# A two-layer decoder trunk on one core: some feed forward input products issued 128 tokens wide instead of 256

## The chip, the cores and the metric

The kernel runs on one core of one Trainium2 chip. The metric is the device time of one execution in microseconds (us). Before the change two executions took 2003.5 and 1999.16 us, with a median of 2001.33 us.

## What is computed

The input is a residual stream of 256 tokens with 2048 features in float32. Layer 0 adds a gated linear recurrence block (RG-LRU) and then a SwiGLU feed forward block. One key and value projection is then taken from the stream, and layer 1 adds a sliding window attention block that uses it, and another SwiGLU block. This case is about the SwiGLU blocks, of which there are two:

```python
D_MODEL = 2048
D_FF = ((8 * D_MODEL // 3 + 255) // 256) * 256      # 5632

def swiglu_ffn(x, g, w_in, w_out):
    h = rms_norm(x, g)
    gate, up = jnp.split(h @ w_in, 2, axis=-1)
    return x + (jax.nn.silu(gate) * up) @ w_out
```

Everything is float32, and every large product is weights (features by features) times the 256 tokens.

## The kernel before

**Layout.** The stream is kept transposed: features on the 128 partitions, the 256 tokens along the free axis. A product therefore holds a 128 by 128 block of weights in TensorE (VectorE, ScalarE and TensorE are named DVE, ACT and PE in the profile) and streams the tokens past it, and the result, 128 features by 256 tokens, accumulates in one PSUM bank of 512 columns.

**Three products instead of one.** A float32 operand is split in two numbers of the type float32r: `hi`, a rounded copy, and `lo`, what the rounding left. A product is then the sum of three: weights `hi` times tokens `hi`, weights `hi` times tokens `lo`, and weights `lo` times tokens `hi`. An activation slot is a tile of 512 columns, with the `hi` half of the 256 tokens in columns 0 to 255 and the `lo` half in columns 256 to 511. The letters of the table `PARTS` (line 259) name such a product: each gives whether the weights are `hi` (1) or `lo` (0), and which columns of the slot are streamed. `a` is `hi` weights with `hi` tokens, `b` is `hi` weights with `lo` tokens, `l` is `lo` weights with `hi` tokens, each 256 columns wide. `h` is `a` and `b` in one instruction of 512 columns; its two halves land in the two halves of the bank and are added when the bank is emptied.

**Jobs and chunks.** All weights come from HBM in one list of jobs, in the order of use. A job is a chunk of 128 by 1024 numbers (512 KB): two blocks of input features (`k`) by four blocks of output features (`f`), so eight blocks of weights. `stream` (line 244) runs over the jobs. For job `i` it issues the DMA of the chunk four jobs ahead (`load`, from the SP queue), splits the chunk three jobs ahead into `hi` (ACT, line 241) and `lo` (DVE, line 242), and then issues the products of job `i`. Four buffers each for the raw chunk, `hi` and `lo` take turns.

**Groups.** `group` (line 273) makes the jobs of four banks that accumulate together. For the feed forward input there are 22 groups in each of the two layers, and each group has eight chunks, `c` from 0 to 7, because its contraction runs over 2048 features. For each chunk, `group` writes the list `todo` of products as triples of `k`, `f` and the letter. In chunks 0, 2 and 5 (`SYNC`) some `a` and `b` pairs are an `h`. In chunk 7 the products are sorted by bank, so that the first bank is done early. In chunks 1, 3, 4 and 6 the list has `a` and `b` for each of the eight blocks, and then `l` for each of the eight: 24 products of 256 columns.

**Issue.** `products` (line 261) turns the list into instructions. Each entry is one matmul call, and the build makes of each call a weight load (LDWEIGHTS, the profile's engine row PEld) and a MATMUL (row PE). Halfway through the list it calls `half_tick` once.

**The rest of the work.** Normalization, SiLU, splitting of activations, attention and the like run as generators in the background. `run_bg` issues their steps at the ticks, so many per tick as budgets of estimated DVE and ACT time allow; these budgets and the ticks do not depend on how many products a chunk has. `done` empties a group's banks with `pull` after chunk 7. The output projection of the feed forward (`project`) uses `group` as well.

The lines that matter here:

```python
                if not self.started:
                    self.started = True
                    todo = [(k, f, p) for k in range(2) for q in ("ab", "l") for f in range(4) for p in q]
                elif c == nk // 2 - 1:
                    todo = [(k, f, p) for f in range(4) for k in range(2) for p in "abl"]
                else:
                    run = [(0, 0), (1, 0), (0, 1)] if c in sync else []
                    todo = [(k, f, p) for k, f in both if (k, f) not in run for p in "ab"]
                    ...
                    todo += [(k, f, "l") for k, f in both]
```

Of the kernel before, what the change touches and what calls it, by code (L numbers as in the profile page):

```python
# [17 lines left out]
P = 128  # L18
D = 2048
T = 256  # L20
DFF = 5632
ND = D // P
NH = DFF // P
# [25 lines left out]
class Trunk:  # L49
# [206 lines left out]
            self.run_bg()  # L256
        self.drain()

    PARTS = {"h": (1, 0, 2 * T), "a": (1, 0, T), "b": (1, T, 2 * T), "l": (0, 0, T)}

    def products(self, todo, ps, hi, lo, x2, begun, last):


        for n, (k, f, p) in enumerate(todo):
            if 2 * n in (len(todo), len(todo) + 1):
                self.half_tick()
            high, c0, c1 = self.PARTS[p]
            w = (hi if high else lo)[:, k * 512 + f * P:k * 512 + f * P + P]
            self.nc.tensor.matmul(ps[f][:, 0:c1 - c0], w, x2[k][:, c0:c1], start=f not in begun,  # L269
                                  stop=last and all(q[1] != f for q in todo[n + 1:]))  # L270
            begun.add(f)

    def group(self, src, nk, xs, done, last=False, sync=()):


        st = {}
        both = [(k, f) for k in range(2) for f in range(4)]
        for c in range(nk // 2):
            def mm(hi, lo, c=c):
                if c == 0:  # L280
                    st["ps"] = [self.bank() for _ in range(4)]
                    st["begun"] = set()
                x2 = [self.need(xs[2 * c + kt]) for kt in range(2)]
# [3 lines that stand above are left out]
                elif c == nk // 2 - 1:  # L287

                    todo = [(k, f, p) for f in range(4) for k in range(2) for p in "abl"]
                else:  # L290
                    run = [(0, 0), (1, 0), (0, 1)] if c in sync else []
                    todo = [(k, f, p) for k, f in both if (k, f) not in run for p in "ab"]
                    at = sync.index(c) if run else 0
                    todo[at:at] = [(k, f, "h") for k, f in run]
                    todo += [(k, f, "l") for k, f in both]
                self.products(todo, st["ps"], hi, lo, x2, st["begun"], c == nk // 2 - 1)
                if last:
                    for q in x2:
                        self.free(q)
                if c == nk // 2 - 1:  # L300
                    done([(p, bool(sync) and f < 2) for f, p in enumerate(st["ps"])])
            self.jobs.append((src(c), mm))
# [111 lines left out]
    def ffn(self, l, xs, r, gains, rn, out=None):  # L414
        hid = [Val() for _ in range(NH)]
        w = self.d[f"ffn_in{l}"]
        for g in range(NH // 2):
            def done(ps, g=g):
                rs = self.rstd[r][:, 0:T]
                early = not self.rv[r].ready  # L420
                v = [self.pull(p, r=None if early else rs) for p in ps]

                def task():
                    while not self.rv[r].ready:
                        yield 1
                    for h in range(2):
                        ga, up = v[2 * h], v[2 * h + 1]
                        if early:
                            self.tt(ga, ga, rs, ALU.mult)
                            self.tt(up, up, rs, ALU.mult)  # L430
                        self.a(ga, ga, AF.Silu)
                        yield
                        self.tt(ga, ga, up, ALU.mult)
                        while not self.slots:
                            yield 1
                        s = self.slot()
                        self.split_act(s, ga)
                        self.free_half(ga)
                        self.free_half(up)
                        hid[2 * g + h].ap = s  # L440
                        hid[2 * g + h].ready = True
                        yield
                self.spawn(task())
            self.group(lambda c, g=g: w[g, c], ND, xs, done, g == NH // 2 - 1, self.SYNC)
        self.project(self.d[f"ffn_out{l}"], NH, hid, gains, rn, out)


# [562 lines left out]
```

## Time and profile before

| what | value |
|---|---|
| median of two runs | 2001.33 us (1999.16 to 2003.5) |
| the profiled execution, its own time | 1999.26 us |
| its span, first to last instruction | 1997.5 us |
| PE busy | 1987.8 us, 16795 matmuls |
| PEld busy | 1955.1 us, 16795 weight loads |
| DVE busy | 1282.1 us (64%) |
| ACT busy | 1077.6 us (54%) |
| granted TensorE clock | 1.000 |
| line 269 (`products`) | 15927 of the matmuls: 10423 with `hi` weights, 5504 with `lo` weights |

The profile is of one execution on the chip. A matmul record of PE begins when the instruction starts to stream, and its end is modelled, so that records of neighbours overlap: a matmul of 256 columns is shown with 276 ns, though the next one starts after less than half of that. The number to read is therefore the distance from one start to the next. A row of the timeline merges neighbours of the same kind: it gives the start, the time from the first start to the last end, and how many there are; the distance is that time less one record, divided by the count less one. A window row gives for each engine the busy time and the number of instructions in a stretch of the span.

### The profile page before, as it was taken

The numbers are of one execution on the slowest core, as the hardware profiler recorded it, in microseconds if no ns is written. First come the engines' busy times: TensorE is split into PE (matmuls) and PEld (weight loads), VectorE is DVE, ScalarE is ACT, GpSimd is POOL, SyncE is SP. The second block draws the span as 40 slices with busy tenths as digits, with TensorE's granted clock in tenths as the row PEclk, the third lists the DMA queues.
The fourth block names the chain that finished last, engine by engine and source line by source line (L and its number), as shares of the span: only waits on it lengthen the run. The fifth ranks groups of instructions, "written<-read, shape, count | busy, mean of one in ns | idle before, by whom it ended". The sixth has DMA issues, their size and how long they took to land.

```text
span 1997.5 us, 40277 instructions
## 1 busy us (share of the span) xinstructions
PE 1987.8 (100%) x16795; PEld 1955.1 (98%) x16795; DVE 1282.1 (64%) x2062; ACT 1077.6 (54%) x1624; POOL 0.2 (0%) x4
## 2 busy tenths in 40 slices
PE   8999999999999999999999999999999999999999
PEld 8999999999999999999999999999999999999999
DVE  8989867556556656545768786765565566554543
ACT  7798655445444444434556775554454454444342
POOL 0000000000000000000000000000000000000000
PEclk9999999999999999999999999999999999999999
DMA  7655655655656566566564335655655665666663
GB/s 268 199 183 177 202 195 188 196 191 190 200 191 197 193 192 198 191 193 197 192 189 141 122 116 169 191 194 191 195 191 195 195 195 191 195 195 202 206 204 128
DMA packets 105015, 376.58 MB, mean 189 GB/s; under 512 B 11648, under 2 KB 13824, under 8 KB 104832
## 3 DMA queue, kind: packets, MB, share of 16 engines
q1 hardware_dynamic: 104832, 374.01, 58.1%
q8 instruction: 131, 2.15, 0.4%
q14 instruction: 52, 0.43, 0.1%
HBM read 371.86 MB, written 2.10 MB: 187 GB/s over the span
## 4 chain that ended last, share of the span: by engine, by line
PE 99%; ACT 0%; DMA 0%; DVE 0%; issue 0%
PE b L269 94%; PE b L545 1%; PE b L832 1%; PE b L740 1%; PE b L895 0%; PE b L851 0%; PE b L784 0%; PE b L786 0%; PE b L785 0%; PE b L853 0%; PE b L852 0%; PE b L749 0%; PE b L750 0%; PE b L751 0%; DMA x<-in_x 0%; ACT hi L241 0%
## 5 line engine op out<-in xcount | busy, mean ns | idle before, releaser
L269 PE MATMUL b<-s,hi 128*128 128x256 f32 (+1 forms) x10423 | 1430.2, 284 | 6.6 <-ACT hi L241 5.7
L269 PEld LDWEIGHTS b<-s,hi 128*128 128x128 f32 x10423 | 1322.5, 188 | 33.9 <-ACT hi L241 6.0
L242 DVE TENSOR_TENSOR lo<-raw,hi 128x1024 fp32r<-128x1024 f32 (+1 forms) x705 | 861.0, 1222 | 661.6 <-ACT hi L241 658.1
L241 ACT ACTIVATE hi<-raw 128x1024 fp32r<-128x1024 f32 (+1 forms) x705 | 746.1, 1059 | 774.7 <-PE b L269 744.3
L269 PE MATMUL b<-s,lo 128*128 128x256 f32 x5504 | 824.4, 277 | 0.0
L269 PEld LDWEIGHTS b<-s,lo 128*128 128x128 f32 x5504 | 716.4, 188 | 0.0
L105 ACT ACTIVATE t<-b 128x256 f32<-128x256 f32 x130 | 48.8, 384 | 62.2 <-PE b L269 37.9
L105 ACT ACTIVATE h<-h 128x256 f32<-128x256 f32 (+1 forms) x104 | 38.9, 375 | 21.1 <-DVE h L114 21.1
L105 ACT ACTIVATE s<-h 128x256 fp32r<-128x256 f32 (+1 forms) x106 | 42.7, 413 | 13.4 <-DVE h L114 10.9
L105 ACT ACTIVATE s<-s 128x256 f32<-128x256 f32 (+1 forms) x112 | 41.2, 415 | 4.0 <-DVE s L118 3.3
L114 DVE TENSOR_TENSOR h<-b,rstd 128x256 f32<-128x256 f32 x102 | 41.6, 415 | 0.0
L105 ACT ACT_TABLE_LOAD x31 | 39.8, 1283 | 1.3 <-PEq L1000 0.7
L114 DVE TENSOR_TENSOR h<-h,rstd 128x256 f32<-128x256 f32 x92 | 38.3, 420 | 1.5
L118 DVE SCALAR_TENSOR_TENSOR s<-x,par,s 128x256 fp32r<-128x256 f32 x80 | 36.7, 479 | 3.9 <-ACT s L105 3.9
L105 ACT ACTIVATE s<-x,par 128x256 fp32r<-128x256 f32 x80 | 37.9, 497 | 2.3 <-DVE x L114 1.8
L114 DVE TENSOR_TENSOR h<-b,t 128x256 f32<-128x256 f32 x90 | 37.5, 417 | 0.0
L114 DVE TENSOR_TENSOR s<-s,s 128x256 fp32r<-128x256 f32 (+1 forms) x80 | 31.0, 419 | 8.8 <-ACT s L105 8.6
L114 DVE TENSOR_TENSOR s<-h,s 128x256 fp32r<-128x256 f32 x88 | 36.6, 417 | 0.0
L114 DVE TENSOR_TENSOR h<-h,h 128x256 f32<-128x256 f32 x88 | 36.4, 415 | 0.1
L105 ACT ACTIVATE s<-b 128x384 f32<-128x384 f32 (+3 forms) x70 | 28.4, 428 | 10.3 <-PE b L853 5.6
L105 ACT ACTIVATE s<-s,h 128x128 f32<-128x128 f32 x64 | 28.3, 444 | 6.2 <-DVE h L123 6.2
L114 DVE TENSOR_TENSOR x<-x,b 128x256 f32<-128x256 f32 x64 | 25.2, 415 | 8.9 <-PE b L269 8.9
(99 smaller groups left out, 610.4 us busy)
## 6 DMA issues: line engine op xcount, KB each, us to landing
raw<-in_ffn_in SPq DMA_DIRECT2D x352, 512.0 KB, 3.5
raw<-in_ffn_out SPq DMA_DIRECT2D x176, 512.0 KB, 4.2
raw<-in_lru_in SPq DMA_DIRECT2D x63, 512.0 KB, 3.8
raw<-in_lru_out SPq DMA_DIRECT2D x32, 512.0 KB, 3.4
raw<-in_w_q SPq DMA_DIRECT2D x32, 512.0 KB, 3.3
raw<-in_w_o SPq DMA_DIRECT2D x32, 512.0 KB, 3.5
raw<-in_gate SPq DMA_DIRECT2D x8, 512.0 KB, 4.0
raw<-in_kv SPq DMA_DIRECT2D x8, 512.0 KB, 4.3
```

Source lines behind the costliest of these rows:

```text
L105: self.nc.scalar.activation(out, in_, func, **kw)
L114: self.nc.vector.tensor_tensor(out, a, b, op)
L118: self.nc.vector.scalar_tensor_tensor(out, a, s, b, op0, op1)
L241: self.nc.scalar.activation(hi[:, q], raw[:, q], AF.Copy)
L242: self.nc.vector.tensor_tensor(lo[:, q], raw[:, q], hi[:, q].bitcast(F32), ALU.subtract)
L269: self.nc.tensor.matmul(ps[f][:, 0:c1 - c0], w, x2[k][:, c0:c1], start=f not in begun, stop=last and all(q[1] != f for q in todo[n + 1:]))
L545: nc.tensor.matmul(ps[j][:, 0:T], (hi if high else lo)[:, c:c + P], x2[kt][:, q:q + T], start=kt == 0 and high > q, stop=kt == 1 and not high)
L740: nc.tensor.matmul(ps[f][:, 0:T], w0, x2[kt][:, q:q + T], start=k0 + kt == 0 and high > q, stop=k0 + kt == ND - 1 and not high)
L832: nc.tensor.transpose(p[:, j * P:(j + 1) * P], sc[hh][:, j * P:(j + 1) * P], one)
```

## The change

Ten letters stand in `PARTS` for products now. `p`, `q`, `r` and `s` are `hi` weights with the first and second 128 tokens of the `hi` half (`p`, `q`) and of the `lo` half (`r`, `s`). `m` and `n` are `lo` weights with the first and second 128 tokens of the `hi` half. `products` writes a narrow product to the half of the bank's columns that its tokens belong to (`o0`).

`FORMS` holds six orders. A form is a tuple of strings; for each string the eight blocks are gone through, and for each block the letters of the string. In chunks 1, 3 and 6 of each feed forward input group the list `todo` is made from a form; which one is `(g + l) % 6`, with the group `g` and the layer `l`. Chunks 0, 2, 4, 5 and 7, and all other stages, keep their lists. The same sums are computed.

```diff
-    PARTS = {"h": (1, 0, 2 * T), "a": (1, 0, T), "b": (1, T, 2 * T), "l": (0, 0, T)}
+    PARTS = {"h": (1, 0, 2 * T), "a": (1, 0, T), "b": (1, T, 2 * T), "l": (0, 0, T),
+             "p": (1, 0, P), "q": (1, P, T), "r": (1, T, T + P), "s": (1, T + P, 2 * T), "m": (0, 0, P), "n": (0, P, T)}
+
+    FORMS = (("pqrsmn",), ("ambn",), ("ab", "mn"), ("a", "m", "b", "n"), ("armns",), ("ab", "m", "n"))
 
     def products(self, todo, ps, hi, lo, x2, begun, last):
...
             high, c0, c1 = self.PARTS[p]
             w = (hi if high else lo)[:, k * 512 + f * P:k * 512 + f * P + P]
-            self.nc.tensor.matmul(ps[f][:, 0:c1 - c0], w, x2[k][:, c0:c1], start=f not in begun,
+            o0 = c0 % T
+            self.nc.tensor.matmul(ps[f][:, o0:o0 + c1 - c0], w, x2[k][:, c0:c1], start=f not in begun,
                                   stop=last and all(q[1] != f for q in todo[n + 1:]))
...
-    def group(self, src, nk, xs, done, last=False, sync=()):
+    def group(self, src, nk, xs, done, last=False, sync=(), form=None):
...
                     todo = [(k, f, p) for f in range(4) for k in range(2) for p in "abl"]
+                elif form is not None and c in (1, 3, 6):
+                    todo = [(k, f, p) for q in self.FORMS[form] for k, f in both for p in q]
                 else:
...
-            self.group(lambda c, g=g: w[g, c], ND, xs, done, g == NH // 2 - 1, self.SYNC)
+            self.group(lambda c, g=g: w[g, c], ND, xs, done, g == NH // 2 - 1, self.SYNC, (g + l) % 6)
```

## The prediction

> **What bounds the kernel now.** I read the page's shares and chain first, then who PE waited for, then windows over the two stages that the diff touches, and last the timeline inside one chunk.
>
> ```profile
> span 1997.5 us, 40277 instructions
> PE 1987.8 (100%) x16795; PEld 1955.1 (98%) x16795; DVE 1282.1 (64%) x2062; ACT 1077.6 (54%) x1624; POOL 0.2 (0%) x4
> PEclk9999999999999999999999999999999999999999
> PE 99%; ACT 0%; DMA 0%; DVE 0%; issue 0%
> PE b L269 94%; PE b L545 1%; PE b L832 1%; PE b L740 1%; PE b L895 0%; PE b L851 0%; PE b L784 0%; PE b L786 0%; PE b L785 0%; PE b L853 0%; PE b L852 0%; PE b L749 0%; PE b L750 0%; PE b L751 0%; DMA x<-in_x 0%; ACT hi L241 0%
> ```
>
> The chain that ended last is PE for 99%, and line 269, the products, for 94%. The clock is full throughout.
>
> ```profile
> L269 PE MATMUL b<-s,hi 128*128 128x256 f32 (+1 forms) x10423 | 1430.2, 284 | 6.6 <-ACT hi L241 5.7
> L269 PE MATMUL b<-s,lo 128*128 128x256 f32 x5504 | 824.4, 277 | 0.0
> L241 ACT ACTIVATE hi<-raw 128x1024 fp32r<-128x1024 f32 (+1 forms) x705 | 746.1, 1059 | 774.7 <-PE b L269 744.3
> L242 DVE TENSOR_TENSOR lo<-raw,hi 128x1024 fp32r<-128x1024 f32 (+1 forms) x705 | 861.0, 1222 | 661.6 <-ACT hi L241 658.1
> ```
>
> These groups show the direction of waiting: PE stood idle 6.6 us before the products of `hi` and not at all before those of `lo`, while ACT waited 744.3 us for PE to give back `hi` buffers.
>
> Windows over the two input stages (columns: busy us and count for PE, PEld, DVE, ACT, POOL; then clock, DMA share, GB/s):
>
> ```profile
> 281.50:759.30 477.80, 477.80 (x4013) 469.61 (x4012) 293.02 (x407) 238.20 (x315) 0.00 (x0) 1.00 0.60 194
> 1258.00:1735.40 477.40, 477.40 (x4007) 469.19 (x4006) 292.36 (x405) 237.69 (x314) 0.00 (x0) 1.00 0.60 194
> ```
>
> In these two windows, together 955.2 us, PE has no idle time, DVE is busy 61%, ACT 50%, the DMA engines 60%. Nothing but the pace of PE's own instructions sets the time there. That pace is read from one chunk, PE's timeline (start, us from first start to last end, count):
>
> ```profile
> 802.38 1.07 PE L269 MATMUL b<-s,lo 128*128 128x256 f32 x8
> 803.29 1.98 PE L269 MATMUL b<-s,hi 128*128 128x256 f32 x16
> 805.10 1.07 PE L269 MATMUL b<-s,lo 128*128 128x256 f32 x8
> ```
>
> From the first `lo` product of one chunk to that of the next are 805.10 − 802.38 = 2.72 us, and 24 products: **113.3 ns a step** at 256 columns. As a check, the stage: 44 groups of 8 chunks of 2.72 us are 957 us, the length of the two windows.
>
> **The change part by part.**
>
> *How many products.* A chunk before has 24, all 256 wide. Form 0 (`pqrsmn`) has 48, all 128 wide: 24 more. Form 4 (`armns`) has 8 wide and 32 narrow: 16 more. Forms 1, 2, 3 and 5 have 16 wide and 16 narrow: 8 more. Over the 22 groups of layer 0 and, shifted by one, of layer 1, the forms 0 to 5 come 7, 8, 8, 8, 7 and 6 times, in three chunks each. Added instructions: 3 × (7×24 + 8×8 + 8×8 + 8×8 + 7×16 + 6×8) = 3 × 520 = **1560**. Each is the second half of a product that was whole, so 1560 steps of 256 columns go and 3120 of 128 columns come; the columns streamed are the same. The change costs 3120 × t − 1560 × 113.3 ns = 3120 × t − 176.8 us, and all hangs on t, the step of a narrow product.
>
> *The step t.* The trace has no float32r product narrower than 256, so t is bounded by rows. If a step took only as long as its columns, it would be half of 113.3: 56.7 ns. But every matmul carries its own weight load: the page counts 16795 of both, although an `a` and the `b` behind it use the same block, so repeated weights are loaded again. What a load costs shows where almost nothing is streamed, at line 895, two columns against 128 columns of weights (timeline of PEld), and, in the groups by shape, in the records of loads:
>
> ```profile
> 1106.00 1.87 PEld L895 LDWEIGHTS b<-con,s 128*128 128x128 f32 x16
> ...
> L269 PEld LDWEIGHTS b<-s,lo 128*128 128x128 f32 x5504 | 716.4, 188 | 0.0
> L832 PEld LDWEIGHTS b<-con,s 128*128 128x128 f32 x96 | 11.3, 140 | 0.9 <-issue 0.5 <-DVE s L114 0.2
> L853 PEld LDWEIGHTS b<-s,s 128*64 128x64 f32 x64 | 7.9, 137 | 0.0
> L895 PEld LDWEIGHTS b<-con,s 128*128 128x128 f32 x64 | 7.5, 191 | 0.0
> ```
>
> Sixteen loads in 1.87 us with a record of 0.19 us: (1.87 − 0.19) / 15 = **112 ns from load to load**, for products of two columns. So the load alone holds PE to one matmul in 112 ns. Its record, 191 ns, is that of the products' loads, 188 ns; a load of 64 columns at line 853 has 137 ns, which gives (188 − 137) × 2 = 102 ns for the part that grows with 128 columns. At 256 columns the stream (113.3) just hides the load (112); at 128 columns the stream (57) hides half of it, and the load sets the step. Line 895 works on plain float32 and the products on float32r, which is why this remains an estimate; the equal records are my reason to carry it over. I take **t = 112 ns**. The low end of this reading is 102 ns. The high end is 117 ns, the pace of wide products while attention runs beside them (six distances in 0.98 − 0.28 us):
>
> ```profile
> 1105.30 0.98 PE L269 MATMUL b<-s,hi 128*128 128x256 f32 x7
> ```
>
> The sum: 3120 × 112 ns = 349.4 us, less 176.8, **+172.6 us**. The ends: +141 at 102 ns, +188 at 117 ns.
>
> The Trainium skill, "TensorE: Matmul & The Clock Gate", section "LDWEIGHTS (loading the stationary operand)", puts a load at its column count over 1.2 GHz whatever the contraction, so 107 ns for 128 columns; the trace's 112 is a little longer. By the Trainium skill's figure the sum would be +157 us and the time 2156, as an estimate.
>
> *Does anything hide it?* PE has no idle time in these windows for the extra steps to fall into, so all of it lies on the path.
>
> *Order of `hi` and `lo`.* Forms 0, 1, 3 and 4 mix `lo` and `hi` weights. A `lo` block is then wanted from the second to the ninth or so product on, instead of the 17th, and the `hi` buffer is read nearly to the end of the chunk. The split three chunks ahead hides both. Within the chunk above:
>
> ```profile
> 802.58 1.06 ACT L241 ACTIVATE hi<-raw 128x1024 fp32r<-128x1024 f32 x1 [1.66 <-PE b L269]
> ...
> 803.67 1.23 DVE L242 TENSOR_TENSOR lo<-raw,hi 128x1024 fp32r<-128x1024 f32 x1 [1.50 <-ACT hi L241]
> ```
>
> ACT refills a `hi` buffer just after its last product and DVE is done with `lo` at 804.90; three whole chunks (8.2 us) lie between the chunk that gave the buffer back, which ended at 803.29, and the one that needs it, at about 811.4. Release up to 0.9 us later, at the end of the chunk, leaves some 5 us. I cost it at nothing. Behind ACT's waiting split stand the background's activations and the bank evictions, and DVE's subtraction; if the cover were gone, each us late would be one us on PE in each of up to 132 chunks. A longer chunk widens the cover.
>
> *The rest.* `half_tick` still runs once in mid list, so ACT, DVE and SP get the same instructions in the same order, with no DMA added or moved; no new kind of wait arises. Transfers are needed less often, and the 60% DMA share falls. 3120 more PE instructions must be fetched; the fetch queues now move 2.6 MB for 40277 instructions, 64 bytes each, so 0.2 MB more, which I cost at nothing:
>
> ```profile
> q8 instruction: 131, 2.15, 0.4%
> q14 instruction: 52, 0.43, 0.1%
> ```
>
> **The forecast**: the profiled execution took 1999.26 us (1.8 around the span), 2 us under the median of the two runs and inside their spread. 1999.3 + 172.6 = **2172 us**.
>
> **The rivals.**
>
> 1. *The load is hidden even behind 128 columns* (not slower). A float32r load may take half of a float32 one: the only loads of 128 columns with a shorter record, 140 ns, are line 832's transposes. If a load takes 57 ns or less, t is 56.7 and the time 1999. It decides from t = (176.8 + 40) / 3120 = 69.5 ns: below it, the change is within 2% (40 us), which is about what a measurement of this kernel can tell from no change. Against it speaks the 188 ns record of the products' own loads. Chance 0.09. The Trainium skill, "TensorE: Matmul & The Clock Gate", section "Back-to-back issue gap", gives a width formula that puts 55.8 ns at 128 columns; by it the time would be 1997.
>
> 2. *The load is hidden in part*, t midway between 57 and 112, so 84.5 ns: 263.6 − 176.8 = +87, 2086 us. For it: no row shows float32r below 256. Against: line 895 would have to be slow for its type. Chance 0.03. The Trainium skill, in the section just named, has sustained pairs of load and matmul at about 81 ns for 128 columns, without saying the type; by that figure it would be +76, 2075.
>
> 3. *A load of weights already in the array costs nothing*, only a change of block does. A step is 112 where the next product takes another block and 57 or 113 else. Per block before 340 ns; form 0 adds 4×57 + 2×112 − 340 = 112 ns, forms 1, 3 and 5 add 110, form 2 55, form 4 166. Times 168 blocks for form 0, 528 for forms 1, 3 and 5, 192 for form 2 and 168 for form 4: 19 + 58 + 11 + 28 = +116, 2115 us. The wide pairs of today would hide it; that each has its own load record speaks against it. Chance 0.03.
>
> 4. *Load and stream no longer overlap at 128 columns*: t = 112 + 57 = 169, +350, 2350 us. At 256 columns they overlap fully, or the step would be 225. Chance 0.03.
>
> 5. *The change does not reach the chip as written*, the build joining neighbours: 1999 us. The `a` and `b` of today, adjacent and of one block, stay two. Chance 0.01.
>
> **How the numbers follow.** Forecast 0.80, rivals 0.09, 0.03, 0.03, 0.03, 0.01, and 0.01 for a gain, for which I see no row: 40 us would need t below 44 ns, less than the stream alone. The forecast's bounds run from 1999 + 141 = 2140 to 1999 + 188 = 2187; I add the 4 us by which the two runs differ and some margin for steps above 117 where wide and narrow alternate, 2200. The 0.20 outside are the rivals, so the range stays 2140 to 2200. Slower by over 2%: 0.80 + 0.03 + 0.03 + 0.03 = 0.89; within: 0.09 + 0.01 = 0.10; faster 0.01.
>
> **What would show it.** In the changed profile: 18355 matmuls; the two input stages longer by some 86 us each, all other stages as before; PE without idle time there; narrow loads following each other every 112 ns. A changed chunk, 2.72 us now, takes 48 × 112 = 5.38 us in form 0, 8 × 113.3 + 32 × 112 = 4.49 in form 4, 3.61 in the others. Rival 3 shows as form 2 shorter than form 5. I would be wrong if narrow products followed each other at well under 100 ns or over 125, or if idle time before products came up, from the earlier use of `lo`.

## The result, and the profile after

The changed kernel took 2198.34 us (2198.17 and 2198.51 in two runs) against 2001.33: a ratio of **1.0991, 95% interval 1.0973 to 1.1008**, slower by 197 us. The profiled execution took 2198.17 us.

From the page of the changed kernel (line 274 is line 269 of before):

```profile
span 2196.4 us, 43409 instructions
PE 2185.6 (100%) x18355; PEld 2151.6 (98%) x18355; DVE 1282.0 (58%) x2062; ACT 1071.6 (49%) x1624; POOL 0.2 (0%) x4
PEclk9999999999999999999999999999999999999999
PE 99%; ACT 1%; DMA 0%; DVE 0%; issue 0%; SPq 0%; DVEq 0%; ACTq 0%
L241 ACT ACTIVATE hi<-raw 128x1024 fp32r<-128x1024 f32 (+1 forms) x705 | 745.6, 1058 | 994.3 <-PE b L274 937.8
```

PE bounds the kernel as it did, at the full clock. There are 1560 more matmuls and as many more weight loads; DVE and ACT have the same 2062 and 1624 instructions in nearly the same busy time. ACT waits longer for PE (937.8 us, 744.3 before), so the cover of the splits has grown. Groups by shape:

```profile
L274 PE MATMUL b<-s,hi 128*128 128x256 f32 x9334 | 1358.7, 282 | 7.8 <-ACT hi L241 6.9 <-ACT s L105 0.8
L274 PE MATMUL b<-s,lo 128*128 128x256 f32 x4448 | 689.6, 278 | 0.0
L274 PE MATMUL b<-s,lo 128*128 128x128 f32 x2112 | 342.9, 263 | 0.0
L274 PE MATMUL b<-s,hi 128*128 128x128 f32 x1008 | 184.8, 265 | 0.0
```

The narrow products are 2112 + 1008 = 3120, and PE waited for no operand before them. Windows over the two input stages, each from its first product to the first of the next stage (columns as in the prediction):

```profile
299.60:879.90 580.30, 580.30 (x4827) 571.49 (x4826) 294.02 (x408) 236.74 (x317) 0.00 (x0) 1.00 0.54 160
1376.00:1953.60 577.60, 577.60 (x4803) 568.80 (x4802) 293.20 (x406) 236.70 (x315) 0.00 (x0) 1.00 0.54 161
```

PE is still without a gap. The stages are 580.3 and 577.6 us long; between the same two products before they were 480.3 and 480.6. Together that is 960.9 to 1157.9 us, **+197.0: nearly the whole loss is there**. The two profiled executions are 198.9 us apart, and what the stages leave of it, 1.9 us, is less than the 4.3 us between the two executions before. One changed chunk of form 5 and its neighbours, timeline of PE and the loads of the same narrow row:

```profile
516.60 2.04 PE L274 MATMUL b<-s,hi 128*128 128x256 f32 x16
518.49 1.90 PE L274 MATMUL b<-s,lo 128*128 128x128 f32 x16
```

```profile
518.37 1.87 PEld L274 LDWEIGHTS b<-s,lo 128*128 128x128 f32 x16
```

Sixteen narrow loads take 1.87 us, (1.87 − 0.19) / 15 = **112 ns apart**, as line 895's were before. Over all narrow products of the trace that follow a narrow one, the distance is 111.6 ns. This leaves out the first distance of each row: the second record begins only 58 ns after the first. In turn the second wide product behind a row begins about 170 ns after the first one. Together that is what two full steps take, so I read it as records that begin early, before their weights are in; the trace does not show this by itself. But the sixteen wide products take 2.04 us where they took 1.98: (2.04 − 0.28) / 15 = **117 ns instead of 113.3**. That was not foreseen, and it is not confined to the changed chunks. Mean distance from the first product of a chunk to that of the next, in us, worked out from the traces (chunks in which the background adds matmuls left out):

| chunk | 0 | 1 | 2 | 3 | 4 | 5 | 6 | 7 |
|---|---|---|---|---|---|---|---|---|
| before | 2.73 | 2.72 | 2.73 | 2.72 | 2.72 | 2.73 | 2.72 | 2.72 |
| after, form 0 | 2.80 | **5.31** | 2.87 | **5.31** | 2.88 | 2.75 | **5.31** | 2.88 |
| after, form 4 | 2.81 | **4.47** | 2.87 | **4.47** | 2.88 | 2.75 | **4.46** | 2.88 |
| after, form 5 | 2.82 | **3.62** | 2.87 | **3.62** | 2.88 | 2.82 | **3.62** | 2.88 |

The bold chunks are the changed ones. Chunks whose instructions are the same as before grew too. A part of that is bookkeeping: a chunk behind a narrow one begins about 55 ns early, and its time has that more. The rest is wide products at the slower pace. In the input stages 4786 wide steps take 117.8 ns, where before 165 did; that is 4621 × 4.46 ns = 20.6 us, and the 396 products of 512 columns rose from 228.9 to 231.8 ns, 1.1 us.

### The profile page after: what moved, and what is told of

The parts are those of the page before. It is cut to its first block, busy times and chain, and to the rows that moved or that the text cites. A ratio compares the mean times of both kernels' runs of the same rounds, so it can differ in the third digit from the quotient of the medians.

```text
span 2196.4 us, 43409 instructions
## 1 busy us (share of the span) xinstructions
PE 2185.6 (100%) x18355; PEld 2151.6 (98%) x18355; DVE 1282.0 (58%) x2062; ACT 1071.6 (49%) x1624; POOL 0.2 (0%) x4
## 4 chain that ended last, share of the span: by engine, by line
PE 99%; ACT 1%; DMA 0%; DVE 0%; issue 0%; SPq 0%; DVEq 0%; ACTq 0%
PE b L274 94%; PE b L552 1%; PE b L839 1%; PE b L747 1%; PE b L902 0%; PE b L858 0%; PE b L791 0%; DMA raw<-in_lru_in 0%; PE b L793 0%; PE b L792 0%; PE b L860 0%; ACT hi L241 0%; PE b L859 0%; PE b L756 0%; PE b L757 0%; PE b L758 0%
## 5 line engine op out<-in xcount | busy, mean ns | idle before, releaser
L274 PE MATMUL b<-s,hi 128*128 128x256 f32 (+2 forms) x10927 | 1601.8, 287 | 7.8 <-ACT hi L241 6.9
L274 PEld LDWEIGHTS b<-s,hi 128*128 128x128 f32 x10927 | 1442.2, 188 | 36.4 <-ACT hi L241 7.3
L241 ACT ACTIVATE hi<-raw 128x1024 fp32r<-128x1024 f32 (+1 forms) x705 | 745.6, 1058 | 994.3 <-PE b L274 937.8
L274 PE MATMUL b<-s,lo 128*128 128x256 f32 (+1 forms) x6560 | 1031.3, 273 | 0.0
L274 PEld LDWEIGHTS b<-s,lo 128*128 128x128 f32 x6560 | 891.1, 189 | 0.0
```

Source lines behind the costliest of these rows:

```text
L241: self.nc.scalar.activation(hi[:, q], raw[:, q], AF.Copy)
L274: self.nc.tensor.matmul(ps[f][:, o0:o0 + c1 - c0], w, x2[k][:, c0:c1], start=f not in begun, stop=last and all(q[1] != f for q in todo[n + ...
```

## The experiments

Two questions were open: whether the weight load is really what sets the narrow step, and where the slow wide steps come from. All ratios are against the kernel before on the same chip.

**Is it the load? Fewer tokens per product.**

```diff
-            self.nc.tensor.matmul(ps[f][:, o0:o0 + c1 - c0], w, x2[k][:, c0:c1], ...)
+            d = 64 if c1 - c0 == P else c1 - c0
+            for j in range(0, c1 - c0, d):
+                self.nc.tensor.matmul(ps[f][:, o0 + j:o0 + j + d], w, x2[k][:, c0 + j:c0 + j + d], ...)
```

> Every narrow product is cut once more, into two of 64 tokens, each with its own load of 128 weight columns (6240 instead of 3120, the same sums). If the weight load sets the step, 64 tokens cost what 128 cost, about 111 ns: 3120 more steps, +346 us on the changed kernel's 2198, so 2545 us. Rival: a narrow float32r product streams its tokens at half the pace of a wide one, so that its columns set the step: two of 64 tokens together take what one of 128 took, and the time stays at 2198 us.

It took 2816.7 us in its one execution. The chunks of forms 1 and 3 take 5.36 us, which is 16 × 113.3 + 32 × 111 ns, and the loads of a row (timeline of PEld) stand as far apart as for 128 tokens:

```profile
650.92 3.66 PEld L276 LDWEIGHTS b<-s,lo 128*128 128x128 f32 x32
```

(3.66 − 0.19) / 31 = 112 ns, for half the columns. The rival, a slower stream, is out. But the time is 270 us over what the load rule gave, for another reason: the granted clock. Its mean was 0.897. A chunk of form 0, 96 products of 64 tokens, window and timeline:

```profile
796.50:812.50 16.00, 16.00 (x90) 16.00 (x89) 1.42 (x2) 0.22 (x1) 0.00 (x0) 0.59 0.22 66
```

```profile
797.22 1.06 PE L276 MATMUL b<-s,hi 128*128 128x64 f32 x8
798.11 0.61 PE L276 MATMUL b<-s,lo 128*128 128x64 f32 x4
...
800.32 1.89 PE L276 MATMUL b<-s,hi 128*128 128x64 f32 x8
802.03 1.04 PE L276 MATMUL b<-s,lo 128*128 128x64 f32 x4
```

From 797.22 to 798.11 eight products pass, 111 ns each; from 800.32 to 802.03 eight take 214 ns each. In the clock record of this trace 60 stretches, each a whole multiple of 3.41 us and 580 us together, run at half clock. 580 / 2 = 290 us is the excess; without it the time would be about 2527, near the 2545 of the load rule. The step nearly doubled at half the clock (111 to 214 ns), so the load goes with PE's clock. The Trainium skill, "TensorE: Matmul & The Clock Gate", section "Part 1: The HAM clock gate (the "warmup" mystery)", has a gate that halves the clock after an idle window of about 3.4 us; the length and the half agree with this trace. The idleness does not: here PE had no gap in its records, only 64 columns streamed in the time of 256.

**Is it the load? Fewer weight columns per product.**

```diff
-            self.nc.tensor.matmul(ps[f][:, o0:o0 + c1 - c0], w, x2[k][:, c0:c1], ...)
+            d = 64 if c1 - c0 == P else P
+            for j in range(0, P, d):
+                self.nc.tensor.matmul(ps[f][0:d, o0:o0 + c1 - c0], w[:, j:j + d], x2[k][:, c0:c1], ...)
```

> Every narrow product is issued twice, each time with the first 64 of its 128 weight columns (the other 64 output features are left out and the first 64 are added twice, so the output is not the reference's; the instructions are as many as in the run with 64 tokens). If the weight load sets the step, half a load takes 56 ns and the stream 57, so the pair costs what one narrow product cost: 2198 us, up to 2230 if something is added per instruction. Rivals: columns streamed at half pace, or a fixed price per product, give 111 ns for each, 2545 us.

(The text above is not exact: the second call takes the second 64 weight columns, and adds their result to the first 64 rows of the bank. The sizes are as stated.) It took 2247.54 us in its one execution, 17 us above the top of what was expected, with 6240 narrow products, as many as in the run with 64 tokens. Timeline of PEld, a row of 32:

```profile
528.70 2.04 PEld L276 LDWEIGHTS b<-s,lo 128*64 128x64 f32 x32
```

(2.04 − 0.135) / 31 = 61 ns: half the load, nearly half the step. Half a load (56 ns) and the stream of 128 tokens (57) are too close to say which of them now sets it, and the 3 or 4 ns above both are not explained. Most of the 49 us over the changed kernel's 2198 come from forms 1 and 4, in which a narrow product stands before a wide one. There the wide product's full load has only 57 ns to hide behind: in form 1 a block is 113.3 + 60 + 112 + 113.3 + 60 + 112 = 571 ns, times eight 4.57 us, and 4.58 was measured; in form 4 it is 113.3 + 7 × 60 + 112, times eight 5.16, and 5.16 was measured. So a step is the longer of the stream of one product and the load of the **next**. That settles the price of the narrow products.

**Does one narrow product slow the wide ones?**

```diff
-                elif form is not None and c in (1, 3, 6):
-                    todo = [(k, f, p) for q in self.FORMS[form] for k, f in both for p in q]
+                elif form is not None and c == 1:
+                    todo = [(k, f, p) for k, f in both for p in "ab"] + [(0, 0, "m"), (0, 0, "n")]
+                    todo += [(k, f, "l") for k, f in both[1:]]
```

> As before the change, but in chunk 1 of each feed forward input group one product (weights lo, the first block) is cut into two of 128 tokens: 44 cuts, which by themselves cost 44 x 0.111 = +5 us. Theory: a narrow product leaves PE's wide products at 117.7 instead of 113.3 ns until three products of 512 columns in chunk 5 bring the pace back. Then 75 wide steps a group are slow, 0.33 us, and +15 us come on top: 2021 us (2043 if chunk 5 does not bring it back). Rival: the slow wide steps of the changed kernel come from the mass of narrow work or from what runs beside it, not from one narrow product: 2006 us.

2004.6 us, ratio 1.0025 (1.0016 to 1.0035): +5 us. My theory missed and the rival was right. Chunk 1 takes 2.83 us, 0.11 more, and the chunks behind it 2.72 to 2.73, as before the change. A single pair of narrow products leaves the pace alone.

**Does the slow pace end by itself?**

```diff
-            self.group(lambda c, g=g: w[g, c], ND, xs, done, g == NH // 2 - 1, self.SYNC)
+            self.group(lambda c, g=g: w[g, c], ND, xs, done, g == NH // 2 - 1)
```

> As before the change, no narrow product, but without the products of 512 columns in the feed forward input groups (two of 256 in place of each; the banks are then emptied without the second half). Theory: the slow pace lasts until a 512 product ends it. Layer 0 enters its input stage at the fast pace and keeps it; layer 1 enters it at the slow pace, left by the attention, and keeps it for all 22 groups, 192 x 22 x 4.4 ns = +18 us: 2019 us. Rival: the pace comes back by itself, or depends on what runs beside: 2000 us in both layers.

2035.13 us, ratio 1.0175 (1.0158 to 1.0192): +35 us with no narrow product in it. The windows over the middle of both input stages:

```profile
327.00:777.00 450.00, 450.00 (x3823) 450.00 (x3823) 250.68 (x322) 195.72 (x240) 0.00 (x0) 1.00 0.59 187
1320.00:1770.00 450.00, 450.00 (x3823) 450.00 (x3823) 250.59 (x320) 195.25 (x240) 0.00 (x0) 1.00 0.59 187
```

3823 products in 450 us are 117.7 ns each, in both layers. The pace persists, and in the kernel before it is the products of 512 columns that end it; I was wrong to think that layer 0 would be spared. Its timeline shows where the slow pace begins, in the first group, and that it still holds in the last one:

```profile
309.84 1.98 PE L269 MATMUL b<-s,hi 128*128 128x256 f32 x16
...
313.93 0.59 PE L372 MATMUL b<-acc,con 128*128 128x256 f32 x2
314.36 0.50 PE L374 MATMUL b<-con,acc 128*128 128x1 f32 x4
...
792.98 1.10 PE L269 MATMUL b<-s,lo 128*128 128x256 f32 x8
```

Before the norm's six small products the wide ones take (1.98 − 0.28) / 15 = 113 ns; after them, and to the end of the stage, (1.10 − 0.28) / 7 = 117 ns. So the pace is no property of narrow products: a passage of other products can bring it about, and it stays.

**Does the order of the same products matter?** Three runs in which all forms are one: single pairs (two wide, two narrow for each block), fours (four wide, four narrow), and rows of sixteen. Their three edits stand in one block, with comments added:

```diff
-    FORMS = (("pqrsmn",), ("ambn",), ("ab", "mn"), ("a", "m", "b", "n"), ("armns",), ("ab", "m", "n"))
+    FORMS = (("abmn",),) * 6           # single pairs
+    FORMS = (("ab", "mn"),) * 6        # rows of sixteen
...
+                    todo = [(k, f, p) for i in range(0, 8, 2) for q in ("ab", "mn") for k, f in both[i:i + 2] for p in q]   # fours
```

> The changed kernel with one order in place of the six forms: for each block the wide products a and b, then its two narrow products m and n. 16 narrow products a changed chunk, 132 such chunks, 1056 added products. The load rule gives one added step of about 113 ns each, +120 us. Theory of the pace: what the wide products take afterwards depends on the sum of the steps before them; the single pair of the run with one cut took 57 + 114 + 169 = 340 ns up to the next wide start but one, three wide steps exactly, and left the pace at 113.3. So with single pairs the unchanged chunks stay at 2.72 us: 2119 us. Rival: eight narrow pairs in a chunk slow the wide products in any order: 2146 us, like the run that goes with this one.

> The changed kernel with form 2 alone: all wide products of the chunk, then the sixteen narrow ones in a row. The same products as in the run with single pairs, in another order. Theory of the pace: the row of sixteen leaves the wide products at 117.7 ns, so that the unchanged chunks take 2.81, 2.87, 2.88, 2.82 and 2.88 us, 0.63 us a group more than before, 28 us in all: 2146 us. Rival: the order is of no account, and both runs take the same time.

> The changed kernel with one order for all groups, between the run with single pairs and the run with rows of sixteen: two blocks at a time, four wide products and then their four narrow ones. The same products as in both. If what counts is that a narrow passage adds up to whole wide steps: the two steps more, 111 and 113 ns, are 2.7 ns short of two steps of 113.3, and the question is whether the fast pace bears that. If it does, 2118 us as with single pairs; if it does not, the wide products behind run at 117.7 ns in the changed chunks too, 2140 us as with rows, up to 2150.

| order | time, us | ratio (interval) | chunks 0 to 7, medians, us |
|---|---|---|---|
| pairs | 2118.79 | 1.0586 (1.0571 to 1.0600) | 2.73 3.57 2.78 3.57 2.78 2.73 3.57 2.78 |
| fours | 2140.09 | 1.0697 (1.0681 to 1.0713) | 2.81 3.63 2.80 3.61 2.88 2.75 3.61 2.88 |
| rows | 2140.04 | 1.0690 (1.0676 to 1.0705) | 2.81 3.62 2.86 3.62 2.88 2.75 3.55 2.88 |

The same 1056 added products cost 21 us more in rows and fours than in pairs. Chunk 4, which is the same in all, on the timelines of pairs (first) and rows (second):

```profile
532.91 2.03 PE L274 MATMUL b<-s,hi 128*128 128x256 f32 x16
534.78 1.07 PE L274 MATMUL b<-s,lo 128*128 128x256 f32 x8
```

```profile
536.24 2.10 PE L274 MATMUL b<-s,hi 128*128 128x256 f32 x16
538.17 1.10 PE L274 MATMUL b<-s,lo 128*128 128x256 f32 x8
```

Its eight `lo` products take (1.07 − 0.28) / 7 = 113 ns behind pairs and (1.10 − 0.28) / 7 = 117 behind rows. A pair added 113.3 ns (a group 24.50 us, before 21.78, and 2.72 / 24 = 0.1133). The passage of a pair (57 + 114 + 169 ns) is exactly three fast steps; with four, two of 111 to 113 come in between, a little off, and the pace is lost. That the sum of steps is what counts is the reading that led to these runs, and it foretold pairs and rows.

The traces allow a closer look at it: the time from the last wide product before a narrow row to the second one behind it, in fast steps of 113.33 ns. Pairs take 4.00 steps and keep the fast pace; the first fours of a chunk take 5.98, and the pace is slow behind the last. Rows of 8, 16 and 48 that turned the fast pace into the slow one take 9.92, 17.80 and 49.33. In the run with half the weight columns, the first row of sixteen in a chunk of form 3 takes 10.93 and turns the pace slow, and the second takes 11.01 and turns it fast again. One case does not fit: form 4 of that run has rows of 7.32 steps with a single wide product between them, and the chunks behind are at the fast pace. So the reading stays a likely one, and why the wide products have two paces is not shown by it.

**Can the 512 products bring it back?**

```diff
                     run = [(0, 0), (1, 0), (0, 1)] if c in sync else []
+                    if form is not None and c in (0, 2, 4):
+                        run = both
                     todo = [(k, f, p) for k, f in both if (k, f) not in run for p in "ab"]
-                    at = sync.index(c) if run else 0
+                    at = sync.index(c) if c in sync else 0
...
-                    done([(p, bool(sync) and f < 2) for f, p in enumerate(st["ps"])])
+                    done([(p, bool(sync) and f < (2 if form is None else 4)) for f, p in enumerate(st["ps"])])
```

> The changed kernel, with all eight blocks of chunks 0, 2 and 4 of the feed forward input as products of 512 columns (three blocks in chunks 0 and 2, none in 4, until now; all four banks are then emptied in two halves, off PE's path). Theory: the products of 512 columns end the slow pace if enough of them follow each other; the wide products behind them are back at 113.3 ns in chunks 0, 2, 4 and 5, 0.42 us a group: 2180 us. Rival: they end it only where their number meets the phase, and a longer row is no better: 2198 us.

2187.77 us, ratio 1.0926 (1.0912 to 1.0941): 11 us back, somewhat more than half of what the theory gave. Timeline of a changed chunk behind a row of eight, with its sixteen wide products ahead of the narrow ones:

```profile
533.39 1.98 PE L274 MATMUL b<-s,hi 128*128 128x256 f32 x16
535.20 1.90 PE L274 MATMUL b<-s,lo 128*128 128x128 f32 x16
```

The pace is back here (1.98, not 2.04), but not everywhere: the wide products behind the row of eight are fast in 93 of the 132 chunks that have one. The places are regular. In chunk 0 the row fails in all groups of forms 2 and 5 and in two others, in chunk 2 in all of forms 1 and 4, in chunk 4 in all of form 1. So each side had a part of it: a longer row often ends the slow pace, and where it does hangs on what came before. Slow wide steps in the input stages fall from 4786 to 1881, 13 us. The 512 products cost 233.9 ns in the mean, 7 more than two fast products of 256, in 1188 of them 8.6 us. About 4.7 of this is only moved, the 54 ns of a narrow row that the first 512 product bears in chunks 2 and 4 in place of a wide one, and 2.0 the changed kernel paid already; the rest, some 1.9 us, is new. The two stages together are 11.5 us shorter, 1157.9 to 1146.4.

**A version faster than before?** The trace of before has some 1600 wide steps at the slow pace, where other products throw it off. With 512 products in all but the first group of the recurrent input, and then also in more chunks of the query projection:

```diff
-            self.group(lambda c: w[4 + g, c], ND, xs, done, sync=self.SYNC if g == 1 else ())
+            self.group(lambda c: w[4 + g, c], ND, xs, done, sync=self.SYNC if g else ())
-            self.group(lambda c: w[g, c], ND, xs, done, g == 3, self.SYNC if g == 1 else ())
+            self.group(lambda c: w[g, c], ND, xs, done, g == 3, self.SYNC)
...
-            self.group(lambda c, g=g: w[g, c], ND, xs, done, g == 3, self.SYNC)
+            self.group(lambda c, g=g: w[g, c], ND, xs, done, g == 3, (0, 2, 3, 5, 6))    # the second run only, in attn
```

> The kernel before the change, no narrow product, with the products of 512 columns also in the groups of the recurrent input that had none (all but the first). In the trace of before, wide products there run at 117 to 119 ns between 150 and 250 us. Theory: some 700 steps at 4.4 ns too much can be brought back, at most 3 us: 1997 us. Rival: the gate products between the groups throw the pace off again, or the phase is missed: 1999.6 us.

> No narrow product: the run with more products of 512 columns in the recurrent input, and in the query projection these products in chunks 0, 2, 3, 5 and 6 of each group instead of 0, 2 and 5. The attention's own products throw the pace off again and again there. Theory: slow wide steps end sooner, some 1 to 2 us: 1996 us against about 1998 for the run without. Rival: the next disturbance follows too soon, or the products of 512 columns miss the phase: 1998 us.

The first took 1998.04 us, ratio **0.9981 (0.9972 to 0.9990)**; slow wide steps before 300 us fall from 640 to 184. The second took 1997.91, ratio 0.9980 (0.9972 to 0.9989): no further gain, the rival of that run. Both are faster than the kernel before by two thousandths, clear of the interval though far below 2%. The slow steps do not explain all of it: 456 of them at 4.46 ns are 2.0 us, and the two profiled spans differ by as much (1997.5 and 1995.7 us). The first run's median is 4.5 us below that of the kernel before, 2002.56 us, whose fifteen executions there go from 1998.6 to 2003.9 while the eleven of this kernel lie between 1997.5 and 1998.8. Why the kernel before scatters more is not shown.

## Why the prediction was right

- **What bounds the kernel**: right. No gap in PE's input stages, all of the added work on the path. The two windows that the prediction calls the input stages begin 16 to 17 us too early and end 19 too early (the stages are 298.5 to 778.8 and 1274.3 to 1754.9 us), and its chunk at 802 us belongs to the output projection. Neither did harm: the chunks of the stages take the same 2.72 to 2.73 us.
- **The count**: right, 18355 matmuls and 3120 narrow ones.
- **The step t = 112 ns, carried over from line 895**: right, 111.6 ns from narrow to narrow, and the runs with half the tokens and half the weight columns show that it is the load. The chunks came out at 5.31, 4.46 to 4.47 and 3.58 to 3.64 us for 5.38, 4.49 and 3.61. The Trainium skill, "TensorE: Matmul & The Clock Gate", section "LDWEIGHTS (loading the stationary operand)", gives 107 ns a load as an estimate; this trace has 111.6.
- **The sum, +172.6 us, measured +197**: short by 24. The step that failed is the assumption, made without a word in the sum, that what stays 256 wide stays at 113.3 ns. It went to 117.8 in 4621 more steps, 20.6 us, and 1.1 us went to the 512 products. So the stages grew by 100.0 and 97.0 us, where some 86 each were forecast. What is left of the stages' 197.0, 175.3 us, is 112.4 ns for each added product, where the estimate had 110.6. I had quoted the pace of 117 ns from the attention stage, and used it as a bound for narrow steps; it was the second pace of the wide ones, already in the profile of before. The time, 2198, lies just inside the range, and that is partly luck: the bound gave 2187, and only the margins added to it, 4 us for the two runs and the rest for narrow steps above 117, made it 2200. The narrow steps were at 111.6; it was the wide ones that used the margin up.
- **Order of `hi` and `lo`, fetches, queues at nothing**: right. PE waited for `hi` 6.9 us in all against 5.7, at the start, and not at all for `lo`.
- **The rivals**: the load hidden, wholly or in part (1 and 2), is out by the distance of 112 ns. Weights already in the array at no cost (3) would have made form 2 shorter than form 5; both take 3.62 us. Load and stream one after the other (4) would be 169. The narrow products are there as written (5).

## What to carry to other kernels

A matmul of float32r pays for the load of its own 128 weight columns, 112 ns here, and a stream of 256 columns just hides the load of the product behind it; halve the stream and the step stays. When an engine is bound by its own pace, read that pace where nothing disturbs it and also where something does: two paces in one trace (113.3 and 117.7 ns here) mean that a change can move the untouched instructions from one to the other, and their number may make that the second term of the sum. The order of narrow and wide products can then be worth as much as nearly a fifth of their price (21 of 116 us).

## What the runs showed of the hardware that I had not expected

Wide products of 256 columns run at 113.3 or at 117.7 ns a step, and stay at the one they have for hundreds of microseconds: all of the input stage of a layer in the run without 512 products. Rows of four or more narrow products of 128 weight columns, or the norm's six small ones, lead from the fast pace to the slow one; single pairs do not. Rows of 512 columns lead back in some places: eight of them in 93 of 132 chunks, and the three in chunk 5 of the changed kernel in forms 0, 3 and 4 always, in forms 2 and 5 never, in form 1 once in eight. The records tell the two paces apart: in the trace of before a weight load begins 110 ns before its product at the fast pace and 115 or 116 at the slow one, and the next load begins 2 to 4 ns after that product in both. What in the chip makes the two paces was not found and stays open.

Products of 64 columns, one each 112 ns without a gap in the record, let the clock fall to a half for multiples of 3.41 us: for 509 of the 580 us in groups of forms 0 and 4, where they are most of a chunk, for 72 us in forms 2 and 5, where 32 of them stand in a row, and never in forms 1 and 3. Products of 128 columns at the same rate never did, in 3120 of them.
